# A third place for raw weight pairs, narrower u tiles and the fill's PSUM bank for every fourth down product, in the last feed-forward part of a two-layer transformer kernel

## The chip, the cores and the metric

The kernel runs on one core of a Trainium2 chip. The metric is the device time of one execution in microseconds, as the median of several runs. The core's engines work side by side and wait for each other through semaphores: PE (TensorE, matrix products; its weight loads are PEld), DVE (VectorE), ACT (ScalarE), POOL (GpSimd) and SP (SyncE, which only issues DMAs here). Each engine takes its own instructions strictly in the order in which they stand in its program.

## The reference

Two layers of a transformer block work on 512 tokens (and 256 context tokens) of width 1024. The last layer updates the 512 tokens alone. This document is about the feed-forward part of that last layer, called layer 1:

```
def swiglu(h, w_gate, w_up, w_down):
    return (jax.nn.silu(h @ w_gate) * (h @ w_up)) @ w_down
...
        x = x + gt2 * swiglu(rms_norm(x, g_ffn[l]) * (1 + sc2) + sh2, w_gate[l], w_up[l], w_down[l])
...
    return rms_norm(x, g_final)
```

The hidden width is 2816, so `w_gate` and `w_up` are 1024 x 2816 and `w_down` is 2816 x 1024. Everything is float32.

## The kernel before, in words

**Precision.** Every float32 operand x is split in two: hi = x rounded to the PE's fast format (a copy on ACT), lo = x - hi (a subtraction on DVE). A product is three matmuls: hi·hi, hi·lo, lo·hi (`mm3`, line 90). The method `split` (line 103) makes both parts, so all casts and all splits carry line 103, whatever tile they write. A matmul's first part of weights needs only ACT's cast; the third of the three needs DVE's subtraction as well.

**Passes.** The hidden columns are worked off in pairs of blocks, p = 0 to 10, 256 columns each. A turn p consists of a gate pass (`seven` on `w_gate`), a down part for the turn before (`down(p-1)`), and an up pass (`seven` on `w_up`). Turn 0 is done by `first`, with plain products.

**One pass.** `load_pair` brings a pair of raw weights, 1 MB, by one DMA on SP into a tile called raw (8192 bytes on each of the 128 partitions). `seven` is a 2x2 block scheme of Strassen's kind with seven products (numbers 1 to 7) in place of eight. It needs sums of weight blocks, which `weights` has POOL make in place: `s` (line 1457), then `raw<-raw` (1458), `raw<-s,raw` (1459), and last `raw<-raw` (1465) for product 3. Product 1 and product 2 use blocks as loaded, product 6 needs line 1459, product 5 needs `s`, product 7 needs line 1458, product 3 needs line 1465. Each of the seven weight operands is then split into one slot `w` out of ten that go round. A product is 12 matmuls of 256 columns. Products 1 and 2 accumulate in one bank of a PSUM tile `lg`, 6 and 7 in its other bank, 5 and 3 in the bank `fl` (one tile only), 4 in one of the three banks `mm`. Between them ACT copies partial results out (lines 1486 and 1491), DVE adds (1488, 1495, 1498, 1501) and POOL adds once (1496). The results are tiles `u`.

**Down.** `down(p)` splits two row blocks of `w_down` (tile `rd`, loaded by `load_down`, one place) into four slots `w`, and makes eight products d = 0 to 7, each of 6 matmuls of 512 columns into an `mm` bank, which DVE adds onto the running `x` (`xt`, line 1804).

**What sets the order.** The code is written pass after pass, but the instruction order on each engine is made at build time by a list scheduler, which has a model of the durations and of free buffers, and which mixes the matmuls of the gate pass, the up pass and the down part. That order is then fixed; on the chip the engines only wait. So a change of a buffer count moves instructions on every engine from there on.

Before the change the raw pairs have two places (`raw`, pool `wp`, two buffers), so a pair is loaded into the place of the pair two before it, when the last split of that pair has read it.

Of the kernel before, what the change touches and what calls it, by code (L numbers as in the profile page):

```python
# [9 lines left out]
F32 = mybir.dt.float32  # L10
# [7 lines left out]
P = 128  # L18
D = 1024
KB = D // P  # L20
SX = 512
SC = 256
T = SX + SC
# [23 lines left out]
class Builder:  # L47
    def __init__(self, tc, ctx, a):
        self.tc, self.nc, self.a = tc, tc.nc, a
        self.n = 0  # L50
        self.line, self.dma, self.last = True, None, None
        pool = lambda **k: ctx.enter_context(tc.tile_pool(**k))
        self.cp = pool(name="cp", bufs=1)
        self.sm = pool(name="sm", bufs=6)
        self.wp = pool(name="wp", bufs=2)
        self.ap = pool(name="ap", bufs=1)
        self.lgp = pool(name="lgp", bufs=2, space=PSUM)
        self.mmp = pool(name="mmp", bufs=3, space=PSUM)
        self.flp = pool(name="flp", bufs=1, space=PSUM)
        self.dp = pool(name="dp", bufs=1, space=DRAM)  # L60
# [55 lines left out]
    def raw(self):  # L116
        return self.wp.tile([P, 2048], F32, name=self.nm("raw"), tag="raw", bufs=2)

    def load_cols(self, src, nk, w, per, slots=None, raw=None):

        hs = []
        krow = src.rearrange("(k p) w -> p k w", p=P)
        step = min(nk, (2048 // w) // per * per)
        for k0 in range(0, nk, step):
            kn = min(step, nk - k0)
            r = (raw or self.raw)()
            rv = r[:, 0 : kn * w].rearrange("p (k w) -> p k w", w=w)
            self.queue(rv, krow[:, k0 : k0 + kn, :])
            for s in range(0, kn, per):
                h, l = (slots or self.whl)()  # L130
                n = min(per, kn - s)
                for j in range(n):
                    c = slice(j * w, (j + 1) * w)
                    self.split(h[:, c], l[:, c], r[:, (s + j) * w : (s + j + 1) * w])
                    hs.append((h[:, j * w : (j + 1) * w], l[:, j * w : (j + 1) * w]))
        return hs

    def load_pair(self, src):

        r = self.raw()  # L140
        rv = r.rearrange("p (k w) -> p k w", w=256)
        self.nc.sync.dma_start(rv, src.rearrange("(k p) w -> p k w", p=P))
        return rv
# [1162 lines left out]
    def w_out(self, l, oh, ol):  # L1306

        nc = self.nc
        full = l < DEPTH - 1
        w = self.a["w_out"][l]  # L1310
        e = T if full else SX
        xt = [self.fp.tile([P, e], F32, name=self.nm("xt"), tag=f"x{k}", bufs=1) for k in range(KB)]
# [17 lines left out]
        for dp in range(KB // 2):  # L1330
            rv = self.load_pair(w[:, dp * 256 : (dp + 1) * 256])
            for j in range(2):
                d = 2 * dp + j
# [14 lines left out]
        last = []  # L1348
        r0, r1 = rngs[0]
# [30 lines left out]
        return t.rearrange("p a b -> p (a b)")[:, 0:512]  # L1380

    def utile(self, dt):
        return self.fp.tile([P, T], dt, name=self.nm("u"), tag="u", bufs=8)

    def norm_raw(self, h, x, bc, rng, l, k, s):

# [391 lines left out]
    def ffn(self, l, xt, hs):  # L1778
        nc = self.nc
        full = l < DEPTH - 1  # L1780
        wg, wu, wd = (self.a[n][l] for n in ("w_gate", "w_up", "w_down"))
        npc = FB // 2
        n = (T if full else SX) // 2
# [7 lines left out]
        def down(p, us, rng, s, wd2, ds=range(KB)):  # L1791
            r0, r1 = rng
            last = p == npc - 1
            for d in ds:
                ps = self.mm()[:, 0 : r1 - r0]
                c = slice(d * P, (d + 1) * P)
                self.mm3(
                    ps,
                    [
                        (wd2[j][0][:, c], wd2[j][1][:, c], us[j][0][:, r0:r1], us[j][1][:, r0:r1])  # L1800
                        for j in range(2)
                    ],
                )
                done = nc.vector.scalar_tensor_tensor(
                    xt[d][:, r0:r1], ps, self.gt(l, 1, d, s), xt[d][:, r0:r1], op0=ALU.mult, op1=ALU.add
                )
                if last:
                    self.stat_add(acc, xt[d], rng, d, nc.gpsimd if full or d != KB - 2 else nc.vector)
                    if full and s == 0:
                        nc.sync.dma_start(self.xsc[:, d, r0:r1], xt[d][:, r0:r1])  # L1810
            return done.ins
# [42 lines left out]
        def downs(rng, s, ds):  # L1854
            for d in ds:
                done.append(down(p, us, rng, s, wd2, (d,)))
                if not full:
                    if d == 0:
                        turned.append([self.lg().rearrange("p a b -> p (a b)") for _ in range(2)])
                    self.turn_out(xt, rng, d, turned[-1])  # L1860
                if norm:
                    with self.tc.issue_after(done[-1]):
                        norm.pop(0)()
# [175 lines left out]
```

## Time and profile before

| what | value |
|---|---|
| median of 3 runs | 1524.29 us (1523.75 to 1527.51) |
| the profiled execution | 1526.21 us, of which the span from first to last instruction is 1524.4 us |
| PE busy | 1467.4 us, 96% of the span |
| DVE busy | 1128.9 us, 74% |
| ACT busy | 758.9 us, 50% |
| POOL busy | 554.5 us, 36% |
| HBM traffic | 136 GB/s over the span |

The span's last part, from about 1165 us, is the feed-forward part of layer 1; the loads of turn 4 and of turn 10 are issued at 1243.60 and 1437.00 us. A busy PE is not yet a PE without gaps: the end of a matmul is modelled in the trace, so that a row lasts longer than the time to the next matmul's start. Gaps are therefore read from starts.

### The profile page before, as it was taken

How to read it: one execution, taken by the hardware profiler on the slowest of the kernel's cores; microseconds unless marked ns; L12 is line 12 of the kernel's file. 1: busy time of each engine (PE TensorE's matmuls, PEld its weight loads, DVE VectorE, ACT ScalarE, POOL GpSimd, SP SyncE). 2: the span in 40 equal slices, each digit the busy share in tenths (PEclk: the TensorE clock that was granted, in tenths of full speed). 3: DMA queues.
4: the chain of work that ended last, by engine and by line, in shares of the span. 5: the costliest groups of instructions: out<-in, count | busy, mean ns of one | idle time of the engine just before them, and what ended most of it. 6: DMA issues, size and time to landing. Idle time of an engine off the chain costs nothing.

```text
span 1524.4 us, 25624 instructions
## 1 busy us (share of the span) xinstructions
PE 1467.4 (96%) x9794; PEld 1353.0 (89%) x9794; DVE 1128.9 (74%) x1917; ACT 758.9 (50%) x1539; POOL 554.5 (36%) x471
## 2 busy tenths in 40 slices
PE   6999999999999999999999998999999999999998
PEld 3889977789999999999899988987799999988987
DVE  4966678744978788876887886667849877787775
ACT  3456667632744344444435545666637444343444
POOL 1544444300265655552000035453402443443432
PEclk9999999999999999999999999999999999999999
DMA  9310085851044444446883440065451423223311
GB/s 354 102 56 29 12 286 170 288 193 31 32 135 163 128 140 141 148 141 241 299 309 113 148 160 28 29 197 186 153 166 56 136 87 111 84 84 113 109 57 55
DMA packets 122394, 208.44 MB, mean 137 GB/s; under 512 B 6368, under 2 KB 88032, under 8 KB 117152
## 3 DMA queue, kind: packets, MB, share of 16 engines
q1 hardware_dynamic: 114416, 200.77, 38.6%
q0 software_dynamic: 7856, 6.04, 2.0%
q8 instruction: 77, 1.26, 0.3%
q14 instruction: 45, 0.37, 0.1%
HBM read 180.96 MB, written 25.82 MB: 136 GB/s over the span
## 4 chain that ended last, share of the span: by engine, by line
PE 70%; DVE 12%; issue 5%; ACT 5%; DMA 4%; POOL 4%; SPq 0%; POOLq 0%; DVEq 0%; ACTq 0%
PE mm L90 15%; PE lg L90 13%; PE fl L90 12%; DVE w L103 5%; PE mm L1647 4%; PE mm L1059 4%; PE lg L1647 4%; PE mm L1051 3%; PE fl L255 2%; PE lg L947 2%; ACT w L103 2%; PE lg L955 2%; PE fl L1647 1%; POOL raw L1465 1%; POOL raw L1459 1%
## 5 line engine op out<-in xcount | busy, mean ns | idle before, releaser
L103 DVE TENSOR_TENSOR w<-raw,w 128x512 fp32r<-128x512 f32 (+1 forms) x314 | 282.2, 911 | 88.4 <-ACT w L103 82.2
L103 ACT CAST w<-raw 128x512 fp32r<-128x512 f32 (+1 forms) x314 | 207.0, 676 | 271.7 <-POOL raw L1465 95.5
L90 PE MATMUL fl<-ahi,w 128*128 128x384 f32 (+1 forms) x640 | 154.3, 308 | 0.0
L90 PE MATMUL lg<-ahi,w 128*128 128x384 f32 (+1 forms) x640 | 149.9, 310 | 2.4 <-DVE w L103 1.9
L90 PE MATMUL lg<-th,w 128*128 128x384 f32 (+1 forms) x640 | 149.2, 309 | 3.1 <-ACT u L1486 1.8
L966 POOL TENSOR_TENSOR p<-p,rc 128x768 f32<-128x768 f32 (+2 forms) x84 | 112.2, 1354 | 107.8 <-DVE rc L964 93.7
L90 PE MATMUL mm<-u,w 128*128 128x512 f32 (+1 forms) x576 | 139.5, 378 | 3.1 <-DVE u L103 2.2
L360 POOL TENSOR_TENSOR rs<-ms,mhalf 128x8 f32<-128x8 f32 (+3 forms) x22 | 30.2, 1380 | 289.6 <-DVE ms L356 289.6
L90 PEld LDWEIGHTS lg<-ahi,w 128*128 128x128 f32 x640 | 111.0, 189 | 6.6 <-DVE w L103 3.8
L90 PEld LDWEIGHTS lg<-th,w 128*128 128x128 f32 x640 | 110.7, 189 | 5.4 <-ACT u L1486 2.6
L90 PEld LDWEIGHTS mm<-u,w 128*128 128x128 f32 x576 | 97.1, 189 | 18.5 <-DVE u L103 3.2
L90 PEld LDWEIGHTS fl<-ahi,w 128*128 128x128 f32 x640 | 111.9, 189 | 1.5
L90 PE MATMUL mm<-ahi,w 128*128 128x256 f32 (+1 forms) x448 | 107.1, 330 | 0.0
L90 PE MATMUL fl<-w,ahi 128*128 128x256 f32 x544 | 106.8, 289 | 0.2 <-DVE t L822 0.2
L958 DVE TENSOR_REDUCE neg<-lg 128x1 f32<-128x768 f32 (+2 forms) x96 | 81.5, 852 | 29.9 <-PE lg L955 29.1
L1457 POOL TENSOR_TENSOR s<-raw 128x512 f32<-128x512 f32 x40 | 54.9, 1373 | 132.8 <-DMA raw<-in_w_gate_dram 60.0
L90 PE MATMUL lg<-tl,w 128*128 128x384 f32 (+1 forms) x320 | 98.8, 309 | 0.0
L90 PE MATMUL fl<-alo,w 128*128 128x384 f32 (+1 forms) x320 | 98.7, 309 | 0.0
L90 PE MATMUL lg<-alo,w 128*128 128x384 f32 (+1 forms) x320 | 98.7, 308 | 0.0
L1465 POOL TENSOR_TENSOR raw<-raw 128x512 f32<-128x512 f32 x40 | 61.5, 1537 | 97.5 <-DVE w L103 97.5
L103 DVE TENSOR_TENSOR t<-mm,t 128x512 fp32r<-128x512 f32 x108 | 74.1, 687 | 30.8 <-ACT t L103 29.6
L959 ACT ACTIVATE p<-lg,neg 128x768 f32<-128x768 f32 (+2 forms) x84 | 70.2, 836 | 40.8 <-DVE neg L958 30.3
(373 smaller groups left out, 4033.5 us busy)
## 6 DMA issues: line engine op xcount, KB each, us to landing
raw<-in_w_ada_dram SPq DMA_DIRECT2D x40, 1024.0 KB, 5.0
raw<-in_w_gate_dram SPq DMA_DIRECT2D x22, 1024.0 KB, 5.2
raw<-in_w_up_dram SPq DMA_DIRECT2D x22, 1024.0 KB, 5.2
uh<-uh SPq DMA_DIRECT2D x33, 384.0 KB, 2.8
w<-uh SPq DMA_DIRECT2D x33, 384.0 KB, 4.2
wd<-in_w_down_dram SPq DMA_DIRECT2D x47, 256.0 KB, 5.0
rd<-in_w_down_dram SPq DMA_DIRECT2D x11, 1024.0 KB, 4.8
raw<-in_w_in_dram SPq DMA_DIRECT2D x9, 1024.0 KB, 5.0
```

The lines of the kernel that those rows point to most:

```text
L90: mm = lambda a, b, **k: self.nc.tensor.matmul(out, a, b, skip_group_check=more, **k)
L103: return self.nc.scalar.copy(hi, src).ins, self.nc.vector.tensor_sub(lo, src, hi).ins
L255: end = nc.tensor.matmul(st["ps"][o : o + 32, :], self.ct[:, k0 + i, :], rs[i][:, j], start=(k0 % hold == 0), stop=((k0 + by) % hold == 0) ...
L947: nc.tensor.matmul(o, qt[:, qs], K1[:, kv, k0 : k0 + w], start=True, stop=False)
L958: nc.vector.tensor_reduce(ng, lv, axis=AX.X, op=ALU.max, negate=True)
L959: nc.scalar.activation(pt, lv, AF.Exp, bias=ng, accum_out=den[:, i : i + 1])
L966: nc.gpsimd.tensor_tensor(pt, pt, rc[:, i : i + 1].to_broadcast(list(pt.shape)), op=ALU.mult)
L1051: nc.tensor.transpose(ps[:, col + j * P : col + (j + 1) * P], pt[:, c : c + P], self.ident)
L1059: nc.tensor.matmul(out[:, r], V[:, kb, kv, :], t[:, c], start=first and n == 0, stop=end and n == len(todo) - 1,)
L1457: nc.gpsimd.tensor_add(s1, a21, a22)
L1465: nc.gpsimd.tensor_sub(a12, a12, a11)
L1647: nc.tensor.matmul(ps, w[:, x, c], u[:, y], start=(not more and k == 0 and j == 0), stop=(k == npc - 1 and j == 2), skip_group_check=True,)
```

## The change

Three edits act on layer 1 alone. (1) While `roomy` is set, which `ffn` does for the last layer, every third raw pair goes to a third place, a tile `raw3` in the pool `fp`. (2) In layer 1 the `u` tiles have 512 columns in place of 768, which frees 8 x 1024 bytes a partition, as much as `raw3` takes. (3) The down products d = 3 and d = 7 of all turns but the last go to the `fl` bank instead of an `mm` bank.

```diff
+        self.third, self.roomy, self.narrow = 0, False, False
...
+    def rawp(self):
+
+        self.third = (self.third + 1) % 3
+        if self.third or not self.roomy:
+            return self.raw()
+        return self.fp.tile([P, 2048], F32, name=self.nm("raw"), tag="raw3", bufs=1)
...
     def load_pair(self, src):
 
-        r = self.raw()
+        r = self.rawp()
...
         full = l < DEPTH - 1
+        self.narrow = not full
         w = self.a["w_out"][l]
...
     def utile(self, dt):
-        return self.fp.tile([P, T], dt, name=self.nm("u"), tag="u", bufs=8)
+        return self.fp.tile([P, SX if self.narrow else T], dt, name=self.nm("u"), tag="u", bufs=8)
...
         full = l < DEPTH - 1
+        self.roomy = not full
         wg, wu, wd = (self.a[n][l] for n in ("w_gate", "w_up", "w_down"))
...
             for d in ds:
-                ps = self.mm()[:, 0 : r1 - r0]
+                ps = (self.fl() if d % 4 == 3 and not last else self.mm())[:, 0 : r1 - r0]
```

The number of instructions of each kind stays; the scheduler orders them otherwise, from the middle of layer 1's feed-forward part's first turns on. All lines below the first edit move by 1 to 10 (1457 becomes 1466, 1459 becomes 1468, 1465 becomes 1474, 1804 becomes 1814).

On SP each up load now stands ahead of the down weights `rd` that it followed, and with three places each raw pair waits for the pair three before it, no longer two. At the start gate pair 1 goes ahead of `rd` of turn 0 and of gate pair 0.

**POOL, the sums of turns 7 and 8.** raw_15159 and raw_15495 are the gate pairs of turns 8 and 9, raw_15024 and raw_15360 the up pairs of turns 7 and 8; the number behind `s` is that of the pair's tile of sums. Before:

```order
L1496 TENSOR_TENSOR u_14687<-u_14687 128x256
L1457 TENSOR_TENSOR s_2461_15161<-raw_15159 128x512
L1459 TENSOR_TENSOR raw_15024<-s_2443_15026,raw_15024 128x4x128
L1458 TENSOR_TENSOR raw_15159<-raw_15159 128x4x128
L1465 TENSOR_TENSOR raw_15024<-raw_15024 128x4x128
L1496 TENSOR_TENSOR u_14822<-u_14822 128x256
L1457 TENSOR_TENSOR s_2488_15362<-raw_15360 128x512
L1459 TENSOR_TENSOR raw_15159<-s_2461_15161,raw_15159 128x4x128
L1458 TENSOR_TENSOR raw_15360<-raw_15360 128x4x128
L1465 TENSOR_TENSOR raw_15159<-raw_15159 128x4x128
```

Now:

```order
L1505 TENSOR_TENSOR u_14687<-u_14687 128x256
L1468 TENSOR_TENSOR raw_15024<-s_2443_15026,raw_15024 128x4x128
L1466 TENSOR_TENSOR s_2488_15362<-raw_15360 128x512
L1474 TENSOR_TENSOR raw_15024<-raw_15024 128x4x128
L1467 TENSOR_TENSOR raw_15360<-raw_15360 128x4x128
L1505 TENSOR_TENSOR u_14822<-u_14822 128x256
L1468 TENSOR_TENSOR raw_15159<-s_2461_15161,raw_15159 128x4x128
L1466 TENSOR_TENSOR s_2506_15497<-raw_15495 128x512
L1474 TENSOR_TENSOR raw_15159<-raw_15159 128x4x128
```

Before, the first sum (1457) of the next pair stood ahead of the sum that the present pair's product 6 needs (1459). Now that sum (1468) comes first in its pass, and what follows it is the first sum (1466) of the pair after the next, with the present pair's last sum (1474) behind it.

**PE, from the end of turn 8's up pass on.** mm_15601 is product 4 of the gate pass of turn 9, mm_15630 and mm_15638 are down products d = 0 and 1 of turn 8 (u_15483 and u_15484 are the hi and lo part of that turn's first `u`, w_15622 and w_15623 those of its down weights), lg_15705 is product 1 of the up pass of turn 9 and lg_15504 product 6 of its gate pass. Before:

```order
L90 MATMUL mm_15601<-th_12498,w_15602 128x256
L90 MATMUL mm_15630<-u_15483,w_15622 128x512
L90 MATMUL mm_15638<-u_15483,w_15622 128x512
L90 MATMUL lg_15705<-ahi_8974,w_15699 128x256
L90 MATMUL lg_15705<-alo_8982,w_15699 128x256
L90 MATMUL lg_15504<-th_12495,w_15518 128x256
```

Now:

```order
L91 MATMUL mm_15601<-th_12498,w_15602 128x256
L91 MATMUL mm_15630<-u_15483,w_15622 128x512
L91 MATMUL lg_15705<-ahi_8974,w_15699 128x256
L91 MATMUL lg_15705<-alo_8982,w_15699 128x256
L91 MATMUL mm_15630<-u_15484,w_15622 128x512
L91 MATMUL mm_15630<-u_15483,w_15623 128x512
L91 MATMUL mm_15638<-u_15483,w_15622 128x512
L91 MATMUL mm_15638<-u_15484,w_15622 128x512
L91 MATMUL mm_15638<-u_15483,w_15623 128x512
L91 MATMUL lg_15705<-ahi_8974,w_15699 128x256
```

The last row is the third matmul of the up pass's product 1, the one that needs DVE's part of w_15699. Now it follows 8 matmuls after the first down matmul; before, in this turn, it followed 38. In turns 5, 7 and 9 these rows stood in the present order before, too. What stands ahead of them differs in every turn: from the last matmul of the up pass's product 3 to the first down matmul there were 48 narrow matmuls in these turns and in turns 4, 6 and 8, and there are 36 now in each of the turns 1 to 9, because ten or more matmuls of the next gate pass's product 1 now stand ahead of product 3.

**DVE, from the same product 3 on.** u_15358 and u_15359 are the results of turn 8's up pass, fl_15399 is its product 3, w_15585 and w_15602 are the next gate pass's operands of products 3 and 4. Before:

```order
L1498 TENSOR_TENSOR u_15358<-u_15358,fl_15399 128x256
L1837 TENSOR_TENSOR u_15358<-u_15358,u_15157 128x256
L103 TENSOR_TENSOR w_15585<-raw_15495,w_15585 128x512
L1501 TENSOR_TENSOR u_15359<-u_15359,mm_15466 128x256
L103 TENSOR_TENSOR w_15602<-raw_15495,w_15602 128x512
L1837 TENSOR_TENSOR u_15359<-u_15359,u_15158 128x512
L103 TENSOR_TENSOR w_15623<-rd_15620,w_15622 128x1024
L103 TENSOR_TENSOR u_15484<-u_15358,u_15483 128x512
L103 TENSOR_TENSOR w_15627<-rd_15620,w_15626 128x1024
L103 TENSOR_TENSOR u_15486<-u_15359,u_15485 128x512
L103 TENSOR_TENSOR w_15699<-raw_15696,w_15699 128x512
```

Now:

```order
L1507 TENSOR_TENSOR u_15358<-u_15358,fl_15399 128x256
L1847 TENSOR_TENSOR u_15358<-u_15358,u_15157 128x256
L104 TENSOR_TENSOR w_15585<-raw_15495,w_15585 128x512
L104 TENSOR_TENSOR w_15602<-raw_15495,w_15602 128x512
L1504 TENSOR_TENSOR u_15359<-u_15359,lg_15369 128x256
L104 TENSOR_TENSOR w_15623<-rd_15620,w_15622 128x1024
L104 TENSOR_TENSOR u_15484<-u_15358,u_15483 128x512
L1510 TENSOR_TENSOR u_15359<-u_15359,mm_15466 128x256
L104 TENSOR_TENSOR w_15627<-rd_15620,w_15626 128x1024
L104 TENSOR_TENSOR w_15699<-raw_15696,w_15699 128x512
```

The new list is the one that stood before in turns 5, 7 and 9; the old one stood in turns 4, 6 and 8. Before, the two kinds of turn alternated; now turns 3 to 8 are all alike. On ACT the copy of product 5 out of the `fl` bank now stands behind five casts of the next pair, where it stood behind one; on PE that product 5 begins after all eight down products instead of between them.

## The prediction

> **What bounds the kernel now.** I read the page's busy shares, then the stage table cut at the gate loads, then PE's waits in that stage, and last the timelines of PE, POOL and DVE around one gap.
>
> ```profile
> PE 1467.4 (96%) x9794; PEld 1353.0 (89%) x9794; DVE 1128.9 (74%) x1917; ACT 758.9 (50%) x1539; POOL 554.5 (36%) x471
> 1243.60:1437.00 193.40, 190.62 (x1309) 175.87 (x1309) 149.20 (x225) 82.17 (x152) 77.47 (x60) 1.00 0.30 99
> 1243.60 0.37 SPq L142 DMA_DIRECT2D raw<-in_w_gate_dram  x1
> 1437.00 0.37 SPq L142 DMA_DIRECT2D raw<-in_w_gate_dram  x1
> 1412.66 1.44 PE fl L90 x12
> 1426.38 2.75 PE mm L90 x12
> ```
>
> PE bounds it. The second line is a stretch of six whole turns (length, then busy time of PE, PEld, DVE, ACT, POOL, granted clock, DMA share, GB/s): the clock is full, DVE as the next engine has 149.20 us of work in 193.40. One turn lasts 32.23 us. PE's own work in it, by the code and the last two lines (pieces of the chain), is 14 products of 12 narrow matmuls at 1.44 us and 8 down products of 6 wide ones at 1.38: 31.2 us. So about 1.0 us a turn is gaps, although the table has only 2.8 us of idle time in all six, since matmul ends are modelled; gaps must be read from starts.
>
> ```profile
> PE mm L90 <- DVE u L103: 2.2, 3, 0.9
> PE lg L90 <- DVE w L103: 1.9, 5, 0.5
> PE mm L90 <- DVE xt L1804: 0.3, 1, 0.3
> 1405.78 0.39 PE L90 MATMUL mm<-u,w 128*128 128x512 f32 x1
> 1407.10 0.74 PE L90 MATMUL mm<-u,w 128*128 128x512 f32 x2 [0.93 <-DVE u L103]
> 1407.92 0.86 PE L90 MATMUL mm<-u,w 128*128 128x512 f32 x3
> 1409.17 0.51 PE L90 MATMUL lg<-ahi,w 128*128 128x256 f32 x2 [0.39 <-DVE w L103]
> ```
>
> The first three lines are all that PE waits for in this stage worth naming (total, times, longest). The gap of 1405.78 to 1407.10 is 1.09 us beyond a wide matmul's 0.23; three of them from 1407.92 to 1409.17 leave another 0.55. This is the start of a down part, waiting for the lo part of `u`, and the third matmul of the next up pass's product 1, waiting for the lo part of its weights. By the same count the pair of gaps is 1.3 us at 1341 and 1.4 at 1470, the ends of turns 5 and 9; the turns between have none. With smaller ones (0.6 at 1216, 0.3 at 1279, 0.5 at 1382) and the pieces of 0.1 us that follow each wait, I count 8.2 us from 1184 to 1498.
>
> Why late? Two things meet. First, POOL:
>
> ```profile
> 1371.87 0.37 SPq L142 DMA_DIRECT2D raw<-in_w_gate_dram  x1
> 1375.31 0.37 SPq L114 DMA_DIRECT2D rd<-in_w_down_dram  x1
> 1375.81 0.68 DVE L103 TENSOR_TENSOR w<-raw,w 128x512 fp32r<-128x512 f32 x1
> 1377.99 1.29 POOL L1457 TENSOR_TENSOR s<-raw 128x512 f32<-128x512 f32 x1 [8.01 <-DMA raw<-in_w_gate_dram]
> 1379.24 1.28 POOL L1459 TENSOR_TENSOR raw<-s,raw 128x512 f32<-128x512 f32 x1
> 1394.83 1.29 POOL L1457 TENSOR_TENSOR s<-raw 128x512 f32<-128x512 f32 x1 [4.64 <-DMA raw<-in_w_up_dram]
> 1400.84 1.61 POOL L1465 TENSOR_TENSOR raw<-raw 128x512 f32<-128x512 f32 x1 [2.23 <-DVE w L103]
> ```
>
> The load at 1371.87 is for the next pair; POOL waits for it at 1457, and the present pair's 1459 behind it, whose input was ready at 1376.5 (the split of 1375.81), is 2.8 us late. The next pass repeats it. Second, DVE, from the end of product 3 on:
>
> ```profile
> 1378.21 0.28 PE L90 MATMUL fl<-ahi,w 128*128 128x256 f32 x1
> 1378.53 0.42 DVE L1498 TENSOR_TENSOR u<-u,fl 128x256 f32<-128x256 f32 x1 [1.72 <-PE fl L90]
> 1401.22 0.41 DVE L1498 TENSOR_TENSOR u<-u,fl 128x256 f32<-128x256 f32 x1
> 1401.67 1.07 DVE L1837 TENSOR_TENSOR u<-u,u 128x256 f32<-128x256 f32 x1
> 1403.14 1.29 DVE L103 TENSOR_TENSOR w<-raw,w 128x512 fp32r<-128x512 f32 x2 [0.40 <-ACT w L103]
> 1404.35 0.41 DVE L1495 TENSOR_TENSOR u<-u,lg 128x256 f32<-128x256 f32 x1
> 1404.68 1.22 DVE L103 TENSOR_TENSOR w<-rd,w 128x1024 fp32r<-128x1024 f32 x1
> 1405.82 1.23 DVE L103 TENSOR_TENSOR u<-u,u 128x512 fp32r<-128x512 f32 x1
> 1406.97 0.41 DVE L1501 TENSOR_TENSOR u<-u,mm 128x256 f32<-128x256 f32 x1
> 1407.30 1.21 DVE L103 TENSOR_TENSOR w<-rd,w 128x1024 fp32r<-128x1024 f32 x1
> 1408.43 0.68 DVE L103 TENSOR_TENSOR w<-raw,w 128x512 fp32r<-128x512 f32 x1
> 1404.84 1.65 POOL L1496 TENSOR_TENSOR u<-u 128x256 f32<-128x256 f32 x1 [2.39 <-DVE u L1495]
> 1434.66 0.74 DVE L1837 TENSOR_TENSOR u<-u,u 128x256 f32<-128x256 f32 x1
> 1438.60 0.68 DVE L103 TENSOR_TENSOR u<-u,u 128x512 fp32r<-128x512 f32 x1
> ```
>
> From 1498 at 1401.22 to the end of the last split at 1409.11 are 7.89 us without a pause but one of 0.40 for ACT. PE goes on 0.06 later, at 1409.17. This row of ten instructions hangs on PE's product 3 at its head and holds PE at its foot.
>
> **The change, part by part.** (1) *Third place.* Each load comes one pass earlier. In the new POOL order the sum behind the DMA is that of the pair after the next, and 1459's successor is always ahead of it. Behind it is only the present pair's last sum, which ran at 1400.84 when that load had been in for 6 us (1394.83). So the lateness of 2.8 us goes, and all present gaps were tied to the old order: -8.2 us at most, which I take in full, since the new order's gaps are counted anew below. Lower end of the gain: 0, if POOL, waiting for `s` instead, stays as late.
>
> (2) *Narrow `u`.* The same instructions on the same 512 columns: 0.
>
> (3) *`fl` for d = 3 and 7.* Saves at most the 0.3 us wait for `xt`, inside the 8.2. It makes product 5 wait until DVE has added product 7's bank: between stand a down product, an `mm` product and three narrow matmuls (1.4 + 1.4 + 0.4 = 3.2 us), the adds take 0.74 each (row below). 0, with two adds' time and more to spare; an excess would come each turn.
>
> (4) *The order of PE.* This is where the time goes. Product 3 now stands later: from its end to that third matmul PE has, in turns 2 to 8 at least, 38 narrow and 6 wide matmuls, 38 x 0.12 + 6 x 0.23 = 5.9 us; in the late turns of now it was 50 narrow ones, 7.4 us, and in the good turns 11.6. DVE's list is the one above in each turn. Its head starts 0.20 us after the end of product 3 (1378.21 + 0.12 to 1378.53). What lasts 7.89 above loses the 0.40 pause and 0.41 of the 1837 that POOL's 1465 stretched (1.07, elsewhere 0.74 and followed after 0.66): 7.08. With the 0.06 at the foot: 0.20 + 7.08 + 0.06 = 7.34 against 5.9, a gap of 1.4 us in each turn, where two turns now share one of 1.3 to 1.6. Bounds: if POOL's 1496 no longer falls between the split of `rd` and that of `u` (1.23, elsewhere 0.68), 0.55 less, so 0.85; if 1465 still runs there, 0.8 more, so 2.2. I take 1.4, because 1496 hangs on 1495 in the same place of the same list, and 1465 is freed by (1). Eight such turns: +11.3; the pieces of 0.1 us after each wait, three or four a time as in the lines at 1407.10 and 1409.17: +2.8. Together +14.1 (9.6 to 20.4).
>
> (5) *Other queues.* SP: `rd` now follows the up load, which frees at what was 1371.87, and `rd` was held until 1375.31 by its own place: 0. At the start 1 MB goes ahead of gate pair 0; PE is busy with the projection until 1163: 0. ACT: the copy out of `fl` stands behind five casts. PE needs it 48 narrow matmuls (5.7 us) after the last down product; four casts need slots of that down part and go at 0.52 us each, product 5 ends 3.0 us in: 0, 2 us to spare; more than that is a rival.
>
> ```profile
> L1804 DVE SCALAR_TENSOR_TENSOR xt<-mm,ada,xt 128x512 f32<-128x512 f32 x48 | 35.1, 741 | 4.6 <-PE mm L90 4.5
> 1391.80 0.62 ACT L103 CAST w<-raw 128x512 fp32r<-128x512 f32 x1 [0.49 <-PE lg L90]
> 1398.44 1.14 ACT L103 CAST w<-raw 128x512 fp32r<-128x512 f32 x2
> ```
>
> Sum: -8.2 + 14.1 = +5.9. The profiled execution of 1526.21 us would become 1532.1; the median of the runs lies 1.92 below it, so 1524.29 + 5.9 = 1530.2 us.
>
> **The rivals.** *Faster: the third place heals the bubble.* If DVE's list is done within PE's 5.9 us, the gaps go and 1524.29 - 8.2 = 1516.1 remains, or up to 1519.7 with pieces left. It decides below 0.3 us a turn, for which the list must take 6.2 us in place of 7.3. For it: the good turns, where POOL's 1459 comes first, have no gap. Against: there PE had 11.6 us, and without any stretch the list is still 6.8. A rule of the Trainium skill speaks for this rival: Perfetto Trace Analysis, section "Identifying Performance Opportunities", says that the same gap repeating on the engine that should be full can mean too little SBUF or PSUM for the next tile. By the rule the new place is the cure and 1516.1 the result; the trace agrees that POOL's 8.01 us wait is such a shortage, but the 7.89 us of DVE after it would stand with any number of places.
>
> *Same: DVE's list unstretched.* Gaps of 0.85 a turn, 6.8 + 2.8 - 8.2 = +1.4, so 1525.7; up to 1528.8 when half the turns are stretched. That the change does nothing (POOL waits for `s` as long as for the DMA, PE order or not) falls here as well, 1524.3.
>
> *Much slower: the copy behind five casts.* In the late pass above the first to the fifth cast took 1391.80 to 1399.58, 7.8 us, where PE leaves 5.7. At 1 us of that in each turn beside (4): 1530.2 + 8 = 1538. Against: most of the 7.8 was POOL's late 1459.
>
> **How the numbers follow.** About 0.3% (4.6 us) is what a measurement of this kernel can tell from no change. Forecast, 1528.9 to 1534: 0.48, since its 1530.2 lies close to that bound. Unstretched or nothing, from 1519.7 to 1528.9: 0.31. Healed, 1516 to 1519.7: 0.16. Copy late, beyond 1534: 0.05. So slower 0.53, same 0.31, faster 0.16. The range of 1518.0 to 1534.0 leaves out the late copy and half of the healed case, whose middle is 1517.9. The likeliest case's own range is 1528.9 to 1534.
>
> **What would show it.** Right: gate loads 32.8 to 33.1 us apart in every turn, not 31.5 and 32.6 in turn; in each turn PE waits about 0.5 us for `u` and 0.9 for `w` (line 104) at the start of the down part, seven or more times each; POOL's long waits for raw DMAs gone. Wrong: no wait of PE at that place and turns of 31.3 us (healed); DVE idle before 1507 for long with PE waiting elsewhere, such as for the copy of line 1500 (ACT), or before `fl` for `xt` (part 3).

## The result, and the profile after

| | before | after |
|---|---|---|
| median of 6 runs | 1527.52 us (1523.75 to 1534.04) | 1542.30 us (1538.98 to 1543.97) |
| the profiled execution, its span | 1526.21 us, 1524.4 us | 1541.55 us, 1539.7 us |

The changed kernel takes 1.0092 of the time of before (95% interval 1.0075 to 1.0109), some 14 us more. The direction and the place were forecast; the size, +5.9 us with a range up to 1534.0, was not.

The profile after, first the page's busy shares, then two gate loads on SP (five turns apart), then the waits of PE that grew, over the whole stage (line waited for: total, times, longest):

```profile
PE 1473.1 (96%) x9794; PEld 1355.1 (88%) x9794; DVE 1140.0 (74%) x1917; ACT 759.0 (49%) x1539; POOL 571.7 (37%) x471
1271.43 0.37 SPq L150 DMA_DIRECT2D raw<-in_w_gate_dram  x1
1436.76 0.37 SPq L150 DMA_DIRECT2D raw<-in_w_gate_dram  x1
PE mm L91 <- DVE u L104: 6.4, 8, 1.3
PE lg L91 <- DVE w L104: 3.7, 6, 0.6
PE mm L91 <- DVE u L1510: 1.9, 2, 1.2
PE lg L91 <- DVE u L1497: 1.6, 1, 1.6
```

The instructions are the same in number, but POOL is busy 17 us longer with its 471, and DVE 11 us. From turn 5's on the gate loads are 33.07 us apart, as the prediction had it (32.8 to 33.1), and in turns 3 to 8 PE waits for the lo part of `u` and for the weights of product 1 in each (the prediction had seven or more waits of both kinds; there are 8 and 6). One such turn, on PE, then DVE's list and the two instructions of POOL beside it (timelines):

```profile
1286.63 0.28 PE L91 MATMUL lg<-alo,w 128*128 128x256 f32 x1
1287.56 1.45 PE L91 MATMUL mm<-u,w 128*128 128x512 f32 x5 [0.65 <-DVE u L104]
1289.63 0.50 PE L91 MATMUL lg<-ahi,w 128*128 128x256 f32 x2 [0.62 <-DVE w L104]
1282.16 0.42 DVE L1507 TENSOR_TENSOR u<-u,fl 128x256 f32<-128x256 f32 x1 [1.16 <-PE fl L91]
1282.62 1.08 DVE L1847 TENSOR_TENSOR u<-u,u 128x256 f32<-128x256 f32 x1
1283.61 1.28 DVE L104 TENSOR_TENSOR w<-raw,w 128x512 fp32r<-128x512 f32 x2
1285.15 1.21 DVE L104 TENSOR_TENSOR w<-rd,w 128x1024 fp32r<-128x1024 f32 x1
1286.28 1.22 DVE L104 TENSOR_TENSOR u<-u,u 128x512 fp32r<-128x512 f32 x1
1288.89 0.68 DVE L104 TENSOR_TENSOR w<-raw,w 128x512 fp32r<-128x512 f32 x1
1282.12 1.29 POOL L1467 TENSOR_TENSOR raw<-raw 128x512 f32<-128x512 f32 x1
1285.37 1.58 POOL L1505 TENSOR_TENSOR u<-u 128x256 f32<-128x256 f32 x1 [1.96 <-DVE u L1504]
```

From 1286.63 to 1287.56 PE has one narrow matmul: 0.81 us of gap. Five wide ones from there, at 0.23 each, end at about 1288.7, and the next row stands at 1289.63: some 0.90. With the pieces of 0.1 us behind them a turn loses 1.89 us (33.07 less 31.18 of work, counted from starts). DVE's list runs from 1282.16 to 1289.57, 7.41 us; PE has 5.9 us to put beside it. Two entries are stretched, the product of line 1847 (1.08) and the split of `u` (1.22), each next to a sum of POOL.

Counted from starts as in the prediction, and at equal work left to do on PE, the stage of layer 1's feed-forward part is 13.1 us longer in the profiled executions:

| part of the stage | time lost on PE before, us | after, us | difference |
|---|---|---|---|
| 330 to 300 us of work left (the end of turn 0) | 4.5 | 6.5 | +2.0 |
| 300 to 240 us left (turns 1 and 2) | 0.7 | 4.8 | +4.1 |
| 240 to 45 us left (turns 3 to 8) | 4.9 | 11.2 | +6.3 |
| the last 45 us | 2.5 | 3.2 | +0.7 |

The other 2.2 us between the two spans arise before this stage, where both kernels have the same instructions; runs of the kernel before alone spread over 10 us.

The third place did what it was said to do to POOL's wait. POOL's waits between 1250 and 1450 us, before and then after:

```profile
POOL s L1457 <- DMA raw<-in_w_gate_dram: 37.6, 7, 8.0
POOL s L1466 <- DVE w L104: 23.2, 11, 2.1
```

The first row's wait for DMAs is gone; the first sum now waits for the split that frees its tile `s`. POOL still idles much (its longest waits are now for DVE at lines 1468 and 1505), which costs nothing by itself.

### The profile page after: what moved, and what is told of

The parts are those of the page before. It is cut to its first block, busy times and chain, and to the rows that moved or that the text cites. A ratio compares the mean times of both kernels' runs of the same rounds, so it can differ in the third digit from the quotient of the medians.

```text
span 1539.7 us, 25587 instructions
## 1 busy us (share of the span) xinstructions
PE 1473.1 (96%) x9794; PEld 1355.1 (88%) x9794; DVE 1140.0 (74%) x1917; ACT 759.0 (49%) x1539; POOL 571.7 (37%) x471
## 4 chain that ended last, share of the span: by engine, by line
PE 73%; DVE 11%; DMA 4%; ACT 4%; issue 4%; POOL 3%; SPq 0%; DVEq 0%; POOLq 0%; ACTq 0%
PE mm L91 16%; PE fl L91 14%; PE lg L91 14%; DVE w L104 4%; PE mm L1656 4%; PE mm L1067 4%; PE lg L1656 4%; PE mm L1059 2%; PE fl L263 2%; PE lg L955 2%; PE lg L963 2%; PE fl L1656 1%; ACT w L104 1%; DMA raw<-in_w_ada_dram 1%; DMA raw<-in_w_gate_dram 1%
## 5 line engine op out<-in xcount | busy, mean ns | idle before, releaser
L104 DVE TENSOR_TENSOR w<-raw,w 128x512 fp32r<-128x512 f32 (+1 forms) x314 | 289.6, 933 | 76.8 <-ACT w L104 68.9
L91 PE MATMUL mm<-u,w 128*128 128x512 f32 (+1 forms) x456 | 113.1, 376 | 9.9 <-DVE u L104 6.4
L1466 POOL TENSOR_TENSOR s<-raw 128x512 f32<-128x512 f32 x40 | 66.3, 1659 | 119.9 <-DVE w L104 45.1
L966 DVE TENSOR_REDUCE neg<-lg 128x1 f32<-128x768 f32 (+2 forms) x96 | 81.4, 852 | 31.4 <-PE lg L963 30.5
L91 PEld LDWEIGHTS mm<-u,w 128*128 128x128 f32 x456 | 76.3, 189 | 24.6 <-DVE u L104 8.5
L1468 POOL TENSOR_TENSOR raw<-s,raw 128x512 f32<-128x512 f32 x40 | 55.5, 1388 | 107.8 <-DVE w L104 107.8
```

The lines of the kernel that those rows point to most:

```text
L91: mm = lambda a, b, **k: self.nc.tensor.matmul(out, a, b, skip_group_check=more, **k)
L104: return self.nc.scalar.copy(hi, src).ins, self.nc.vector.tensor_sub(lo, src, hi).ins
L966: nc.vector.tensor_reduce(ng, lv, axis=AX.X, op=ALU.max, negate=True)
L1466: nc.gpsimd.tensor_add(s1, a21, a22)
L1468: nc.gpsimd.tensor_sub(a11, s1, a11)
```

## The experiments

All were timed in turn with the kernel before on the same chip; "ratio" is to it, with a 95% interval. A kernel with the narrow `u` alone has, on every engine, the order of the kernel before, so it was not run.

### Which of the edits? Each alone

`third_only` leaves out the `fl` edit, `fl_only` the third place:

```diff
-                ps = (self.fl() if d % 4 == 3 and not last else self.mm())[:, 0 : r1 - r0]
+                ps = self.mm()[:, 0 : r1 - r0]
```

```diff
-        if self.third or not self.roomy:
-            return self.raw()
-        return self.fp.tile([P, 2048], F32, name=self.nm("raw"), tag="raw3", bufs=1)
+        return self.raw()
```

> The third place and the narrow u alone; all down products in mm banks as before. POOL and SP have the order of the kernel after. Product 3 stands as late as in the kernel after (5.13 us of PE work to the lo part of u, 5.59 to the third matmul of product 1), but the list of DVE is two splits and a product shorter there, 6.0 us. Theory of the row of DVE: a gap of 0.4 to 0.5 us a turn and its pieces, some 1.3 us less a turn than in the kernel after: 1530 to 1532, ratio 1.002 to 1.003. Rival, the third place: 1.008 to 1.010, as in the kernel after. Rival, the fl bank alone costs the time: 0.995 to 1.000.

> The fl bank for down products 3 and 7 alone, with two places for raw pairs; POOL and SP have the order of the kernel before (the narrow u alone leaves every engine's order as it was before). Product 3 stands late on PE in every turn (4.53 to 4.77 us to the lo part of u). Theory of the row of DVE: lists of two kinds in turn; in the odd turns 5.4 us to the lo part of u against 4.53, a gap of 0.9, in the even ones next to none: 4 to 6 us in eight turns, as much as the kernel before loses there, ratio 0.998 to 1.003, unless POOL's late sums make the lists later still. Rival, the fl bank: 1.006 to 1.010. Rival, the third place: 1.000.

Measured: third_only 1.010 (1.0084 to 1.0115), fl_only 1.0137 (1.0121 to 1.0152). Both missed their forecasts, which had counted DVE's list alone; third_only came out where its rival, the third place itself, had it, which is tested further below. Each alone costs as much as both or more, so the prices of the two edits don't add; each makes the scheduler build an order in which PE waits for DVE. In third_only a turn takes 33.65 us, and its list starts with a split that waits 1.51 us for an ACT cast behind POOL's last sum. PE's waits there between 1250 and 1450 us:

```profile
PE mm L91 <- DVE u L104: 6.6, 6, 1.3
PE mm L91 <- ACT u L104: 2.9, 6, 0.5
```

In fl_only the list starts late, too. DVE, POOL and ACT ahead of one list of it (timelines):

```profile
1309.99 1.75 DVE L104 TENSOR_TENSOR w<-raw,w 128x512 fp32r<-128x512 f32 x1 [1.05 <-ACT w L104]
1311.66 1.78 DVE L104 TENSOR_TENSOR w<-s,w 128x512 fp32r<-128x512 f32 x1
1309.89 1.30 POOL L1464 TENSOR_TENSOR s<-raw 128x512 f32<-128x512 f32 x1 [0.59 <-DMA raw<-in_w_up_dram]
1311.27 1.62 POOL L1465 TENSOR_TENSOR raw<-raw 128x512 f32<-128x512 f32 x1
1314.12 1.68 POOL L1472 TENSOR_TENSOR raw<-raw 128x512 f32<-128x512 f32 x1 [1.23 <-DVE w L104]
1315.83 1.14 ACT L104 CAST w<-raw 128x512 fp32r<-128x512 f32 x2 [4.04 <-POOL raw L1472]
1316.48 1.29 DVE L104 TENSOR_TENSOR w<-raw,w 128x512 fp32r<-128x512 f32 x2 [1.50 <-ACT w L104]
1317.69 0.42 DVE L1505 TENSOR_TENSOR u<-u,fl 128x256 f32<-128x256 f32 x1
```

Two splits that last 0.68 alone take 1.75 and 1.78 beside two sums; the pair's last sum (1472) waits for DVE, ACT's cast for that sum, DVE for the cast, and only then the list begins at 1317.69. So I read it as a ring, POOL to ACT to DVE to PE, in which DVE and POOL lengthen one another.

### Is it the cover that PE gives the list?

`p3first` keeps the kernel after and adds one rule on PE: the gate pass's product 1 stands behind the up pass's product 3. PE's cover grows from 5.9 to 7.36 us; DVE's list keeps its instructions and their order.

```diff
-        product(1, a)
+        with self.after(*self.hold):
+            product(1, a)
...
         product(3, c, True)
+        self.third_end = self.last
...
+            self.hold = [self.third_end] if self.roomy and p > 1 else []
             self.seven(wg[:, cols(p)], toks, n, *g, lambda o, ps: nc.scalar.activation(o, ps, AF.Silu))
...
+            self.hold = []
             self.seven(
```

> The kernel after, with one rule on PE: the gate pass's product 1 stands behind the last matmul of the up pass's product 3. POOL, SP and the order of DVE between product 3 and the third matmul of the next up pass's product 1 stay; only PE gets 12 narrow matmuls (1.43 us) more to do between the two (7.36 us in place of 5.93). Theory of the row of DVE (its list of ten instructions is longer than what PE has to do beside it): 7.4 us of list against 7.36, so the gaps of 0.81 and 0.90 us a turn fall to 0.0 to 0.3, some 1.6 us less in each of turns 1 to 9, and 1542.3 becomes 1528 to 1530, a ratio to the kernel before of 1.000 to 1.003. Rival, the third place (POOL's new order and the loads cost the time): no change, 1.009. Rival, the fl bank shared by products 5, 3 and the down products 3 and 7: no change, 1.009.

Measured: 1.0071 (1.0047 to 1.0095), an interval that overlaps that of the kernel after. In the profile a turn went from 33.07 to 32.93 us, the right way, but some 1.6 us were to go. DVE's list and what is ahead of it there:

```profile
1307.02 1.62 POOL L1467 TENSOR_TENSOR s<-raw 128x512 f32<-128x512 f32 x1 [2.12 <-DVE w L105]
1308.59 1.74 POOL L1475 TENSOR_TENSOR raw<-raw 128x512 f32<-128x512 f32 x1
1310.37 1.14 ACT L105 CAST w<-raw 128x512 fp32r<-128x512 f32 x2 [2.99 <-POOL raw L1475]
1309.16 0.42 DVE L1510 TENSOR_TENSOR u<-u,fl 128x256 f32<-128x256 f32 x1
1311.02 1.90 DVE L105 TENSOR_TENSOR w<-raw,w 128x512 fp32r<-128x512 f32 x2 [0.41 <-ACT w L105]
1316.92 0.68 DVE L105 TENSOR_TENSOR w<-raw,w 128x512 fp32r<-128x512 f32 x1
```

The list starts 1.4 us earlier against PE, and in its middle meets splits whose casts wait for POOL's last sum, which stands behind the sum of the pair after the next. It waits 0.41 us, and the two splits take 1.90 where they took 1.28. The list is now 8.44 us long (1309.16 to 1317.60) against 7.36.

`wnext` moves one entry within the list: the split of the next up pair's product-1 weights goes ahead of the add of product 4 and of the second `rd` split.

```diff
+            self.upw = self.begin(wu[:, cols(p)]) if not full else None
             wd2 = load_down(p - 1)
...
+                    with self.after(*([self.lo11] if self.lo11 and s else [])):
-                    self.split(h[:, c], l[:, c], r[:, (s + j) * w : (s + j + 1) * w])
+                        self.split(h[:, c], l[:, c], r[:, (s + j) * w : (s + j + 1) * w])
```

(`begin` loads the up pair and makes that split, behind the lo part of `u`; `lo11` is the split.)

> The kernel after, with DVE's split of the next up pair's product-1 weights moved ahead of two instructions of the list (the add of product 4 and the second split of rd), right behind the lo part of u; PE's order stays but for a few down matmuls. Theory of the row of DVE: the wait of 0.90 us for w at the third matmul of product 1 goes with its pieces, that of 0.81 us for u stays: 0.9 to 1.0 us less in 8 or 9 turns, 1542.3 becomes 1533 to 1535, ratio 1.004 to 1.005. Rival, the wait only moves to the second split of rd, which is now later: 1.008 to 1.010. Rivals third place and fl bank: no change, 1.009.

Measured: 1.013 (1.0115 to 1.0146), worse. The wait for `w` went, and a larger one came that neither text had: the add of product 4 and the second product with `g`, now later, make the second `u`, and ACT's cast of it holds the next down matmuls.

```profile
PE mm L92 <- ACT u L105: 9.7, 6, 1.6
```

`p3first_sum` adds to p3first that the sum of the pair after the next stands behind the present pair's last sum on POOL.

```diff
+        with self.after(*(self.sums[-2:-1] if self.roomy else [])):
-        nc.gpsimd.tensor_add(s1, a21, a22)
+            nc.gpsimd.tensor_add(s1, a21, a22)
...
-                    nc.gpsimd.tensor_sub(a12, a12, a11)
+                    self.sums.append(nc.gpsimd.tensor_sub(a12, a12, a11).ins)
```

> p3first with one more rule, on POOL: the first sum of the pair after the next stands behind the present pair's last sum (L1474 in the kernel after). In p3first that last sum ran 1.6 us late behind the other, ACT's casts waited for it, and DVE's list took 8.44 us where it took 7.41. New theory, a ring of POOL, ACT, DVE and PE: the last sum is 1.3 to 1.6 us earlier, the list is back at 7.3 us or less, and PE has 5.96 us to the lo part of u and 6.67 to the third matmul of product 1: no wait for u, 0.5 to 0.8 us for w; a turn 0.7 to 1.0 us shorter than p3first's 32.93, ratio to the kernel before 1.001 to 1.003. Rival, DVE's row alone, POOL's order immaterial: PE's cover at w is 0.69 us less than in p3first, so 1.007 to 1.011. Rival, the third place itself: 1.007 or more.

Measured: 1.0131 (1.0111 to 1.0151). The last sum did come earlier, but the other two now run beside the list: the pair of splits took 2.39 us in place of 1.28. The split for product 1 took 1.21 in place of 0.68, beside POOL's add (line 1505 before, 1509 here), and PE waited there.

```profile
1318.29 2.39 DVE L106 TENSOR_TENSOR w<-raw,w 128x512 fp32r<-128x512 f32 x2
1323.80 1.21 DVE L106 TENSOR_TENSOR w<-raw,w 128x512 fp32r<-128x512 f32 x1
PE lg L93 <- DVE w L106: 8.9, 6, 1.5
```

### Is it POOL beside DVE's list?

These two leave part of POOL's work out. In turns 3 to 8 they keep the order of the instructions but for one add of the gate pass (line 1510) that stands one place earlier on DVE. `thin5` cuts the add of line 1505, `thin57` the sum of line 1467 as well:

```diff
-        (nc.vector if n > 256 else nc.gpsimd).tensor_add(c22, c22, c21)
+        cc = slice(0, n if n > 256 else 8)
+        (nc.vector if n > 256 else nc.gpsimd).tensor_add(c22[:, cc], c22[:, cc], c21[:, cc])
...
-        nc.gpsimd.tensor_sub(a21, a11, a21)
+        tn = slice(0, 4 if self.roomy else P)
+        nc.gpsimd.tensor_sub(a21[:, :, tn], a11[:, :, tn], a21[:, :, tn])
```

> The kernel after with POOL's add of line 1505 cut to 8 of its 256 columns in layer 1 (the rest of that add is left out); the order of the instructions stays but for a few adds onto xt. In the kernel after this add ran beside DVE's split of u, which took 1.22 us there and 0.68 elsewhere. Theory, POOL's sums stretch DVE's list: the split of u falls to 0.68, the gaps of 0.81 and 0.90 us a turn to 1.2 together, 0.5 us in 8 or 9 turns: 1542.3 becomes 1537 to 1538.5, ratio to the kernel before 1.006 to 1.007. Rival, the list's length in instructions alone counts, its stretch is chance: 1.009.

> thin5 with POOL's sum of line 1467 cut as well, to 4 of its 128 columns in each block (the rest of it is left out). In the kernel after that sum ran beside DVE's product of line 1847 (1.08 us, 0.42 without POOL beside it). Theory, POOL's sums stretch DVE's list: it falls from 7.41 to 6.2 us against PE's 5.93, the gaps from 1.71 to 0.5 us in each turn: 10 us less in 8 or 9 turns, 1531 to 1533, ratio 1.002 to 1.004. Rival, length in instructions alone: 1.009. Rival, a new wait takes the place: 1.006 or more.

Measured: thin5 1.006 (1.0039 to 1.0081), thin57 1.002 (1.0004 to 1.0035), both as the theory had it. The split of `u` in thin5, the product of line 1847 (here 1849) in thin57, and PE's waits of thin5 and of thin57 between 1250 and 1450 us:

```profile
1316.53 0.69 DVE L104 TENSOR_TENSOR u<-u,u 128x512 fp32r<-128x512 f32 x1
1310.90 0.42 DVE L1849 TENSOR_TENSOR u<-u,u 128x256 f32<-128x256 f32 x1
PE lg L91 <- DVE w L104: 4.4, 7, 0.6
PE lg L91 <- DVE w L104: 2.7, 7, 0.4
```

1.22 became 0.69 and 1.08 became 0.42. The wait for `u` (4.6 us in this window in the kernel after) is gone from the waits in both, and a turn lasts 32.54 and 31.90 us, 0.53 and 1.17 less than 33.07. That is what the entries shrank by: 0.53, and 0.53 + 0.66 = 1.19 us. So the list's end sets the turn, and POOL's work beside it is 1.2 of the 1.89 us that a turn loses.

### Does the third place cost, or the order that came with it?

`up3_nofl` has the third place, no `fl` edit, and the up pass's product 1 behind down product 3. `p3first_nofl` is p3first without the `fl` edit, `p3first_b` the same with two places.

```diff
-        product(1, a)
+        with self.after(*self.hold):
+            product(1, a)
...
+                self.dend[d] = self.last
...
+            self.hold = [self.dend[3]] if self.roomy else []
             self.seven(
```

> Third place and narrow u, no fl bank for down products, and one rule on PE: the up pass's product 1 stands behind down product 3. PE then has 10.03 us from product 3's end to the down part and 22.99 to the third matmul of product 1, in all turns. Ring theory: DVE's list of 6 to 8 us fits, no wait for u or w at the down part; 0.993 to 0.998. Rival, the third place itself costs (POOL's sums and loads in their new order): 1.005 or more. Rival, the gap only moves to the next operand that POOL, ACT and DVE make late (product 5, 6 or 3 of a pass): a wait of PE for w in lg or fl of 0.5 us or more each turn, 1.000 to 1.008.

> Third place and narrow u, no fl bank for down products, and the rule of p3first. PE has 7.4 and 8.79 us in one kind of turn and 5.96 and 11.62 in the other. Ring theory: lists of 6 to 8.4 us; at most 0.5 us of wait for u in every second turn, none for w: 0.995 to 1.000. Rival, the third place itself: 1.005 or more. Rival, DVE's list as long as in p3first (8.44) in every turn: waits of 0.6 us for u in each turn, 1.002 to 1.005.

> Two places for raw pairs, mm banks for all down products, narrow u: the kernel before with the rule of p3first alone. PE has 7.4 and 8.79 us in the turns that had 5.96 and 7.36, the others stay at 5.96 and 11.62. Ring theory: the gaps of 1.3 to 1.6 us at the ends of turns 5, 7 and 9 shrink by up to 1.4 us each, 3 to 4 us in all: 0.997 to 0.998, unless POOL's wait for the DMA grows with it (then 1.000). Rival, only a third place can take the waits away: 0.999 to 1.001.

Measured: up3_nofl 1.0298 (1.0272 to 1.0324), p3first_nofl 1.0021 (1.0011 to 1.0031), p3first_b 1.0008 (0.9995 to 1.0021). All three missed their forecasts; p3first_b came out as its rival had it. up3_nofl gives the list all the time it needs, and loses in another place (and by a low clock, see the last section). PE's largest wait there between 1250 and 1450 us:

```profile
PE mm L92 <- DVE u L1513: 14.3, 6, 2.9
```

That is DVE's add of product 4, whose `mm` bank a down product needs; DVE stands at a split for ACT ahead of it. In p3first_nofl the turns take 31.4 us, 0.2 over the bare work, and the time is lost in turns 0 to 2, where the third place begins, and after the last turn.

`late3_10` is p3first_b with the third place from turn 3 on; the orders of PE, DVE and ACT stay but for turns 2 and 3, and POOL and SP have the new one. `q3_10` is the kernel before with narrow `u` and the third place from turn 3 on, with no rule.

```diff
-        self.roomy = not full
+        self.roomy = False
...
+            self.roomy = not full and 3 <= p <= 10
             g = [self.utile(F32) for _ in range(2)]
```

> p3first_b (two places, mm banks, the gate pass's product 1 behind product 3) with the third place from turn 3 on. PE, DVE and ACT keep p3first_b's order but for 110 matmuls and 25 DVE rows of turns 2 and 3; only POOL's and SP's order are new. Theory, a third place takes POOL's wait for the DMA away and does no harm where PE's order leaves DVE's list its time: p3first_b's gaps of 1.0, 1.6, 2.0 and 1.2 us at the ends of turns 3, 5, 7 and 9 fall to 0.3 each or less, 4 to 5 us less, ratio to the kernel before 0.996 to 0.998. Rival, the third place itself costs: 1.003 or more. Rival, it does nothing: 1.000 to 1.001.

> The kernel before with narrow u and a third place from turn 3 on, no rule on PE and no fl bank for down products: PE has 7.4 and 8.79 us in turns 5, 7 and 9 and 5.84 and 12.93 in turns 4, 6 and 8, so product 3 does not come late everywhere as when the third place begins in turn 1. Theory of the orders (whether the third place helps or hurts hangs on where product 3 falls): gaps of 0 to 0.4 us in every second turn, none in the others: 0.996 to 0.998. Rival, the third place itself costs: 1.003 or more.

Measured: late3_10 0.9982 (0.9968 to 0.9996), q3_10 0.9986 (0.9968 to 1.0004). Against third_only (1.010), q3_10 differs only in the turn in which the third place begins, and thereby in the order from then on. POOL's wait for DMAs, and PE's waits of two kinds, between 1250 and 1450 us, first in p3first_b, then in late3_10:

```profile
POOL s L1465 <- DMA raw<-in_w_gate_dram: 25.8, 7, 6.1
PE mm L92 <- DVE u L1511: 2.6, 3, 1.3
PE lg L92 <- DVE u L1497: 1.1, 3, 0.4
```

```profile
POOL raw L1469 <- DMA raw<-in_w_up_dram: 1.1, 1, 1.1
PE mm L92 <- DVE u L1513: 1.3, 3, 0.8
```

With the same order on PE, DVE and ACT the third place takes the 25.8 us of POOL's waits away and 2.4 of PE's 3.7; two turns that answer to each other (from 1346.30 and from 1343.98) take 62.83 us in place of 64.13. So the place is worth something by itself, 1.3 us in these two turns, where the order leaves the list its time. late3_10, at a median of 1525.97 us, is the only version whose interval lies below 1.000, and by little; that of q3_10 takes in 1.000.

### What makes the start late?

In the kernel after the first sum of turn 2's gate pair now lies on POOL where DVE splits the tokens without a pause. POOL, ACT and DVE there:

```profile
1174.25 10.33 POOL L1466 TENSOR_TENSOR s<-raw 128x512 f32<-128x512 f32 x1 [11.07 <-DVE w L104]
1185.96 1.45 POOL L1474 TENSOR_TENSOR raw<-raw 128x512 f32<-128x512 f32 x1
1187.44 1.14 ACT L104 CAST w<-raw 128x512 fp32r<-128x512 f32 x2 [3.24 <-POOL raw L1474]
1183.35 0.41 DVE L1536 TENSOR_TENSOR acc<-acc,mm 128x256 f32<-128x256 f32 x1
1183.68 2.60 DVE L104 TENSOR_TENSOR tl<-u,th 128x256 fp32r<-128x256 f32 x2
```

A sum of 1.3 us took 10.33; behind it the present pair's last sum and ACT's cast are late, two splits of DVE that elsewhere take 0.75 together take 2.60, and PE waits 1.6 us for line 1497 right after, a gap of 1.73 us where the kernel before has 0.63. Two kernels move that sum and its successor, and no other instruction on any engine: `start_sum` behind the last sum of turn 1's gate pair, `start_late` behind the next one, the sum of line 1468 of turn 1's up pair.

```diff
+        with self.after(*(self.sums[-2:-1] if self.second else [])):
-        nc.gpsimd.tensor_add(s1, a21, a22)
+            nc.gpsimd.tensor_add(s1, a21, a22)
...
+            self.second = not full and p == 2
```

(`sums` holds the sums to stay behind, `second` marks turn 2's gate pair; start_late takes `self.sums[-1:]`, the sums of line 1468.)

> The kernel after with one rule on POOL, for one sum: the first sum (line 1466) of turn 2's gate pair, and with it the second (1467), stand behind the last sum (1474) of turn 1's gate pair. These three rows of POOL are the only ones of the whole program that change places. Theory, the sum that took 10.33 us beside DVE's splits of the tokens is what makes the start 2.0 us longer: the last sum runs by 1183 in place of 1186, the gap of 1.73 us at the end of turn 0 falls to 0.6 to 0.7 as in the kernel before, the stage becomes 1 to 2 us shorter, ratio to the kernel before 1.0075 to 1.009. Rival, DVE's splits make whatever sum stands there wait as long, so the last sum itself takes 10 us: the gap stays at 1.7 or grows, 1.009 or more. Rival, the start is late for another reason: no change in the gap.

> As start_sum, with the two sums of turn 2's gate pair one step later on POOL: the first of them (1466) stands behind the sum (1468) that turn 1's up pair needs, after the dense stretch of DVE; five rows of POOL change places against the kernel after, and nothing on another engine. In start_sum the two sums still ran beside DVE's last pair of token splits, which took 2.61 us (1.52 before, with one sum beside it), and the gap of 1.73 us stayed. Theory, sums beside that pair of splits make the gap: the pair falls to 1.5 us, the gap at the end of turn 0 to 0.6 to 0.7, and the stage is 1 to 2 us shorter than in the kernel after, unless the same sums stretch the split of rd or the list right behind it, then 0 to 1. Rival, the start is late for another reason: the gap stays at 1.7. The ratio to the kernel before, 1.0075 to 1.009, tells little; the gap in the profile decides.

Measured: start_sum 1.0089 (1.0068 to 1.0110), start_late 1.0084 (1.0063 to 1.0105); two us in 1540 are too little for the ratio to tell. DVE's pair of splits in start_sum, and in start_late:

```profile
1180.90 2.61 DVE L105 TENSOR_TENSOR tl<-u,th 128x256 fp32r<-128x256 f32 x2
1184.79 1.52 DVE L105 TENSOR_TENSOR tl<-u,th 128x256 fp32r<-128x256 f32 x2
```

In start_sum no sum takes 10 us any more, and the last sum comes 3 us earlier in the stage, but the gap stayed at 1.73: the two sums run beside the splits all the same. In start_late they don't, the gap is 0.62, and the time lost between 330 and 300 us of work left is 4.4 us, as before the change (4.5). So the start is late because two more sums lie beside DVE's last splits of the tokens, and not because one of them takes 10 us.

## Why the prediction was wrong in size

The forecast of 1530.2 us missed the 1542.3 measured by 12.1. Of these, 3.2 are its starting point: it took the median of three runs of the kernel before, 1524.29, where six gave 1527.52. The other 8.9 are the size of the change, 14.8 us between the medians against 5.9; the profiled executions show 7.2 of them as terms of the sum.

**The old gaps, -8.2 us.** They went, as term (1) had it. At equal work left they were 7.5 us, 0.7 less than I had counted.

**The narrow `u`, 0, and `fl` on PE's waits, 0.** Right: the narrow `u` changes no order, and no wait for the `fl` bank came up in each turn. That the `fl` edit alone costs time (fl_only) comes, as far as its trace shows, through the order.

**The new gap in each turn, 1.4 us and 0.35 of pieces.** Measured 1.71 and 0.18, together 1.89 against 1.75. The list was 7.41 us where the sum had 7.08. The small miss here is the freed stretch of the product with `g`: I took 0.41 off because the sum that ran beside it (1465) would come earlier. It did, and the next sum, 1467, took its place, at 1.08. thin57 shows that price: 0.66. The bound for the other stretch, 0.55, was thin5's 0.53.

**Eight such turns.** This is the mis-sized term: +14.1 was 17.2 for turns 1 to 9. Turns 3 to 8 lose 11.2 us where six of 1.75 make 10.5. Turns 1 and 2 lose 4.8 where two make 3.5; the order in them is not that of the later turns. Turn 9, a ninth that the sum did not count, loses 1.2.

**The start, 0.** Step (5) failed outright: +2.0. I let the earlier loads at the start cost nothing because PE is busy with the projection until 1163. But with the third place turn 2's gate pair is loaded at 1152.73 us, before at 1185.28; its sums come forward with it, and they fall beside DVE's densest stretch (start_late shows that this is the cost). After the last turn come another 1.4 that no step had, where PE waits 1.2 us for DVE's add of line 1510; no run tests why. (In the table's last row turn 9's smaller gap gives 0.7 back.)

0.7, 3.1 (17.2 less 14.1) and 3.4 (2.0 and 1.4) are the 7.2 us between 5.9 and the 13.1 of the profiled executions; the rest of the medians' difference lies before the stage and in the spread of the runs.

**The rivals.** "Healed" was wrong for this order, and right for one that gives the list room (31.4 us a turn in p3first_nofl and late3_10). The rule of the Trainium skill that stood beside it (Perfetto Trace Analysis, "Identifying Performance Opportunities": a repeating gap as a sign of too little SBUF or PSUM) would have given 1516.1; the measurement differs, with more of both the time was 1542.3. "Unstretched" names a cause that thin57 confirms, but the change did not bring it. "The copy behind five casts" did not show: PE has no wait for it.

## What to carry to other kernels

When a buffer is added under a list scheduler, price the order that comes out, engine by engine, and the first turns apart from the steady ones: the same third place measured 1.010 when it began in turn 1 and 0.9986 when it began in turn 3. A turn of a balanced ring is as long as the list of the small engines between one PE product and the next that needs it, so compare that list with the PE work beside it, and don't expect a gap to close by the length of what is moved: in p3first 1.43 us of cover gave 0.14. Price DVE and POOL instructions by what runs beside them, not by their usual duration.

## What the runs showed of the hardware that was not expected

DVE and POOL shut each other out for whole instructions. POOL's add of line 1505 started at 1285.37 while the `rd` split ran to 1286.36, and took 1.58 us; in the gate pass, with no such neighbour when it starts, it takes 0.73 (timeline of the kernel after):

```profile
1303.15 0.73 POOL L1505 TENSOR_TENSOR u<-u 128x256 f32<-128x256 f32 x1 [4.80 <-DVE u L1504]
```

The split of `u` took 1.22 (0.69 in thin5). An estimate from these durations: POOL waits some 0.9 us and runs 0.7, then DVE waits some 0.5 and runs 0.7. The Trainium skill, SBUF — State Buffer, "Who interferes with whom", says that a DVE instruction with two SBUF inputs contends with a GpSimd instruction that reads SBUF, and that such contention is an exclusive lock; the traces agree (0.68 against 1.22, and 10.33 for a sum of 1.3). The adds that read PSUM (lines 1504, 1510) kept 0.40 to 0.42 us in all of these traces.

What was not expected is that POOL got no turn for some 9 us beside the token splits, back-to-back DVE instructions that read both operands from SBUF. By its usual 1.3 us it ran from about 1183.3, when DVE came to line 1536, which reads one operand from PSUM. It is not always so: at 1285.37 POOL did get its turn between two such instructions, the splits of `rd` and of `u`. What decides, no run here shows.

PE's granted clock can fall after a gap. In up3_nofl each of the four gaps that keep two starts 3.3 us apart (3.1 beyond a wide matmul) was followed by a low clock, here in two stretches around one (length, busy time of PE, PEld, DVE, ACT, POOL, clock, DMA share, GB/s):

```profile
1329.00:1333.00 4.00, 1.65 (x9) 0.90 (x7) 2.31 (x5) 0.62 (x1) 1.95 (x2) 1.00 1.06 386
1333.00:1337.00 4.00, 2.90 (x10) 2.22 (x11) 1.98 (x4) 1.16 (x3) 0.00 (x0) 0.73 0.17 71
```

Inside the second the clock goes to 0.50 at 1334.8 us and is back at 1.00 at 1338.2. Such stretches add up to 27.3 us in up3_nofl's stage; at half clock I estimate up to 13.7 us of its loss from them, so a gap can cost more than its length. The length of a gap alone does not decide: a gap of 1.8 us left the clock at 1.00 in wnext and was followed by 0.50 from 1168.5 to 1171.9 us in late3_10, and of four gaps of 2.0 us in up3_nofl two were followed by a low clock. What else decides stays open. The profiled executions of fl_only, wnext, p3first_nofl, start_sum and start_late have one such stretch of 3.4 us at the end of the stage, up to 1.7 us each by the same estimate; those of the kernels before and after have none in the stage.
